# All chunks of U ahead of V, Wr in pieces ahead of its use, and more of the gather beside the routing

## The chip, the cores and the metric

The kernel runs on one core of a Trainium2 chip. A core has TensorE (PE) for matmuls, VectorE (DVE), ScalarE (ACT) and GpSimd (POOL) for the rest, and SyncE (SP), which here only issues DMAs; ACT and POOL issue some too. Each engine takes its instructions in order. The metric is the device time of one execution in microseconds (us).

## What is computed

The program is two transformer blocks over 512 tokens of width 1024. The change lies in the feed-forward of the first block, a mixture of 16384 experts with product keys:

```python
s = jnp.einsum('tpcd,pckd->tpck', q, sub_keys)      # 8 heads, 2 x 128 keys
...                                                   # top 16 of the sums: idx, top
g = jax.nn.softmax(top, axis=-1)
a = jax.nn.gelu(jnp.einsum('tpkd,td->tpk', u[idx], t))
return jnp.einsum('tpk,tpkd->td', g * a, v[idx])
```

Every token takes 8 x 16 of the 16384 rows of U and V (1024 wide, float32).

## The kernel before

The first 128 tokens (T0) are done by **gathering**: an indirect DMA on POOL (L1136) fetches one row of U or of V for each of the 128 tokens, 512 KB a load, 128 loads from each table. DVE multiplies a U row by the token's h (L1155, result `dots`) and adds a V row, weighted, to `accg` (L1160). Two loads and two such instructions are a pair of the generator `gathered`.

The other 384 tokens (TD) are done **densely**: all 16384 experts are worked through as 128 chunks of 128. For a chunk, `hidden` loads 512 KB of U (`w`, L1339), splits it into a high part on ACT (`wh`, L1342) and a low part on DVE (`wl`, L1343), runs 24 matmuls with 384 columns against the tokens (`hh`, `hl` of the pool h2, 32 KB a partition) and takes the gelu (`act`, L1351). `ahead` writes it to DRAM (`Ad`, L1357, 192 KB). Later `operands` reads it back (L1368), multiplies it by the routing weights `Wr` (L1372), splits it (`sh`, `sl`) and V's chunk (`vh`, `vl`, L132 and L134), and `products` adds 18 matmuls with 512 columns to six banks.

The weights come from the **routing**: for each of four blocks of 128 tokens `topk` finds the 16 best on DVE, and `spread` turns a block's choice (not the first's) into dense weights by one-hot products on PE (`go`, `oh`), which go to DRAM as `Wd`. `Wr` is the part of Wd for a group of 8 chunks (GROUP), 1.5 MB in 512-byte pieces, loaded when the first chunk of the group comes up (L1365).

So there are two stages. In the first, routing, 112 U chunks and the first gather pairs are woven together: each generator yields a number, and the one with the least sum goes next. A U chunk yields PACE, a gather pair GATHER; the routing's own numbers add up to 330. PE runs in this written order; the other engines' order is set by a scheduler. Four more U chunks (REST) follow. In the second stage the chunks 0 to 127 go through V; 116 (AHEAD) have their `act` in DRAM, the last 12 run `hidden` there. The remaining gather pairs are spread evenly over the first 120 chunks. Products trail the operands by OPS_LAG chunks.

SP's queue carries the loads of U, V, act and Wr in one order, and an entry that waits holds all behind it. The pool `st` has four buffers `w` (WBUFS) for U and V. `pm` holds Wr, act, sh, sl, vh, vl.

`rows_of` copies a vector that lies along partitions to all partitions as a row: it scales the identity by each of its 8 columns on DVE (`dg`, L372), multiplies by ones on PE and copies the bank (L374). It is used four times: gt1r, a2r, sh2r, and gt2r just ahead of the products with V. The vectors come from `late_mods`, which runs near the start beside the first projection and loads 32 pieces of `wmt` on SP.

Of the kernel before, what the change touches and what calls it, by code (L numbers as in the profile page):

```python
# [7 lines left out]
F32 = mybir.dt.float32  # L8
# [15 lines left out]
AHEAD = 116  # L24
REST = 4
PACE = 2.95
GROUP = 8
WBUFS = 4
# [4 lines left out]
GATHER = 11.0  # L33
OPS_LAG = 2
# [56 lines left out]
class Net:  # L91
# [271 lines left out]
    def rows_of(self, vec, name, pool):  # L363

        nc = self.nc
# [337 lines left out]
    def hg_chunks(self, hg, kv):  # L703
# [17 lines left out]
        for i in range(last + 2):  # L721
# [4 lines left out]
            else:  # L726
# [3 lines left out]
                self.gate = self.rows_of(self.gt1, "gt1r", ha)  # L730
# [290 lines left out]
    def peer(self):  # L1021
# [3 lines left out]
        a2 = self.gain_of(1, self.sc2, 0, "a2")  # L1025
        first = self.proj_first(self.ws, mv, lambda i: self.normed_half(i, [(hh, hl, a2)], 1e-6, self.sh2[:, :, 0]))
# [8 lines left out]
        self.Ad = self.tc.dram_tile([AHEAD, 128, TD], F32, name="Ad")  # L1035
        pg = self.pool("pg", "right")
        self.rows_natural(pg, a2)
        sc = self.queries(mv, first)
        pq = self.pool("pq", "right")
        ac = self.pool("ac")  # L1040
# [4 lines left out]
        gather = self.gathered(pg, ac)  # L1045
        with self.tc.manual_schedule(engines={mybir.EngineType.PE}):
            weave(self.route(pq, pg, sc), steps(ahead, AHEAD - REST), self.until_routed(gather))
# [12 lines left out]
        for e in range(128 + OPS_LAG):  # L1060
            if e < 128:
                ops[e] = self.operands(pm, e, dense)
# [13 lines left out]
        for name in ("pm", "pg", "h2"):  # L1076
            self.shut(name)
# [22 lines left out]
        self.shut("ac")  # L1100

    def rows_natural(self, pg, a2):
# [4 lines left out]
        gain, shift = self.rows_of(a2.unsqueeze(2), "a2r", tmp), self.rows_of(self.sh2, "sh2r", tmp)  # L1107
# [724 lines left out]
```

## Time and profile before

| | us |
|---|---|
| median of 3 runs | 3147.87 (3142.14 to 3153.35) |
| profiled execution, its own time | 3142.09 |
| its span | 3140.3 |
| routing beside U, from about 690 | to 1302 |
| products with V, to the last one | 1302 to 2007 |

The page gives busy time of each engine, a map of the span in 40 slices, the DMA queues, the chain that ended last, and the costliest groups of instructions by line. Busy shares over the whole span mix stages with different limits, so the rows further down are of stretches. A time in brackets is idle time of the engine, with what ended it. A wait for several things is put down to the one that came last; the profile names one DMA where an instruction waits for several.

### The profile page before, as it was taken

The numbers are of one execution on the slowest core, as the hardware profiler recorded it, in microseconds if no ns is written. First come the engines' busy times: TensorE is split into PE (matmuls) and PEld (weight loads), VectorE is DVE, ScalarE is ACT, GpSimd is POOL, SyncE is SP. The second block draws the span as 40 slices with busy tenths as digits, with TensorE's granted clock in tenths as the row PEclk, the third lists the DMA queues.
The fourth block names the chain that finished last, engine by engine and source line by source line (L and its number), as shares of the span: only waits on it lengthen the run. The fifth ranks groups of instructions, "written<-read, shape, count | busy, mean of one in ns | idle before, by whom it ended". The sixth has DMA issues, their size and how long they took to land.

```text
span 3140.3 us, 42392 instructions
## 1 busy us (share of the span) xinstructions
PE 2951.1 (94%) x16073; PEld 2529.5 (81%) x16073; DVE 1898.6 (60%) x3680; ACT 1268.6 (40%) x2275; POOL 401.1 (13%) x398
## 2 busy tenths in 40 slices
PE   7998999999999999898888888899999999999998
PEld 5887887799899999776676767778888887788887
DVE  5744497549999856678788875544433245543323
ACT  4233463343466778522232323432423234433222
POOL 2100000001111110133344431000000000000000
PEclk9999999999999999999999998999999999999999
DMA  6622202236676776899999995222333322123332
GB/s 250 228 64 72 62 1 81 98 126 202 204 239 218 255 248 225 286 353 358 355 363 360 361 353 201 64 72 94 100 95 94 99 86 65 54 88 94 99 103 81
DMA packets 257166, 537.79 MB, mean 171 GB/s; under 512 B 20161, under 2 KB 135105, under 8 KB 252609
## 3 DMA queue, kind: packets, MB, share of 16 engines
q1 hardware_dynamic: 196512, 345.82, 33.8%
q0 software_dynamic: 36864, 134.23, 12.0%
q10 hardware_dynamic: 23584, 55.03, 4.6%
q8 instruction: 126, 2.06, 0.3%
q14 instruction: 80, 0.65, 0.1%
HBM read 484.93 MB, written 50.08 MB: 170 GB/s over the span
## 4 chain that ended last, share of the span: by engine, by line
PE 56%; DVE 19%; DMA 9%; issue 4%; ACT 1%; POOL 1%; SPq 0%; DVEq 0%; ACTq 0%; POOLq 0%
PE bank L121 54%; DMA act<-Ad 7%; DVE wl L1343 2%; DVE gr L1155 2%; DVE accg L1160 2%; DVE vl L134 2%; DVE sl L134 1%; PE bank L608 1%; DVE act L1372 1%; PE bank L1471 1%; DVE idx L1275 1%; DVE tmp L1233 1%; DVE eq L1272 1%; DVE eq L1274 1%; DVE KX L802 1%
## 5 line engine op out<-in xcount | busy, mean ns | idle before, releaser
L121 PE MATMUL bank<-hh,wl 128*128 128x512 f32 (+2 forms) x2304 | 837.0, 364 | 41.8 <-DVE wl L1343 32.3
L121 PE MATMUL bank<-hh,wh 128*128 128x512 f32 (+2 forms) x2304 | 843.0, 367 | 16.2 <-ACT wh L1342 6.8
L121 PE MATMUL bank<-hl,wh 128*128 128x512 f32 (+2 forms) x2304 | 834.5, 362 | 1.5 <-DVE hl L271 0.8
L148 DVE TENSOR_TENSOR wl<-w,wh 128x1024 fp32r<-128x1024 f32 (+2 forms) x280 | 295.0, 1054 | 644.2 <-ACT wh L147 637.5
L147 ACT ACTIVATE wh<-w 128x1024 fp32r<-128x1024 f32 (+2 forms) x280 | 257.5, 920 | 746.1 <-PE bank L121 604.1
L121 PEld LDWEIGHTS bank<-hh,wl 128*128 128x128 f32 x2304 | 437.9, 190 | 101.0 <-DVE wl L1343 42.6
L121 PEld LDWEIGHTS bank<-hh,wh 128*128 128x128 f32 x2304 | 438.1, 190 | 69.9 <-ACT wh L1342 7.6
L121 PEld LDWEIGHTS bank<-hl,wh 128*128 128x128 f32 x2304 | 438.4, 190 | 48.9 <-DVE hl L532 1.6
L121 PE MATMUL bank<-vh,sh 128*128 128x512 f32 x768 | 248.7, 406 | 45.9 <-ACT sh L132 30.8
L121 PE MATMUL bank<-vl,sh 128*128 128x512 f32 x768 | 249.6, 407 | 19.4 <-DVE vl L134 19.2
L1136 POOL DMA_INDIRECT gr<-in_Un_dram,iu x128 | 170.6, 1333 | 735.7 <-DVE accg L1160 493.2
L121 PE MATMUL bank<-vh,sl 128*128 128x512 f32 x768 | 244.3, 400 | 0.0
L132 ACT ACTIVATE sh<-act 128x384 fp32r<-128x384 f32 x128 | 67.1, 525 | 383.4 <-DVE act L1372 347.3
L121 PEld LDWEIGHTS bank<-vh,sh 128*128 128x128 f32 x768 | 149.2, 196 | 80.6 <-ACT sh L132 33.8
L1343 DVE TENSOR_TENSOR wl<-w,wh 128x1024 fp32r<-128x1024 f32 x128 | 156.1, 1221 | 77.3 <-ACT wh L1342 77.3
L1342 ACT ACTIVATE wh<-w 128x1024 fp32r<-128x1024 f32 x128 | 135.1, 1056 | 163.8 <-PE bank L121 144.0
L121 PEld LDWEIGHTS bank<-vl,sh 128*128 128x128 f32 x768 | 149.1, 196 | 59.5 <-DVE vl L134 28.8
L121 PEld LDWEIGHTS bank<-vh,sl 128*128 128x128 f32 x768 | 150.4, 196 | 32.9 <-DVE sl L134 0.2
L1136 POOL DMA_INDIRECT gr<-in_V_dram,iv x128 | 151.4, 1183 | 172.4 <-DVE gr L1155 105.5
L134 DVE TENSOR_TENSOR vl<-w,vh 128x1024 fp32r<-128x1024 f32 x128 | 156.6, 1223 | 13.4 <-ACT vh L132 13.1
L1160 DVE SCALAR_TENSOR_TENSOR accg<-gr,wt,accg 128x1024 f32<-128x1024 f32 x127 | 162.8, 1282 | 0.2 <-DMA gr<-in_V_dram,iv 0.2
L1155 DVE SCALAR_TENSOR_TENSOR gr<-gr,h 128x1024 f32<-128x1024 f32 x128 | 156.0, 1221 | 2.8 <-DMA gr<-in_Un_dram,iu 2.8
(373 smaller groups left out, 4690.9 us busy)
## 6 DMA issues: line engine op xcount, KB each, us to landing
w<-in_U_dram SPq DMA_DIRECT2D x128, 512.0 KB, 4.6
w<-in_V_dram SPq DMA_DIRECT2D x128, 512.0 KB, 6.9
w<-in_wgu_dram SPq DMA_DIRECT2D x84, 512.0 KB, 3.5
Wd<-W ACTq DMA_DIRECT2D x24, 1024.0 KB, 6.8
Wr<-Wd SPq DMA_DIRECT2D x16, 1536.0 KB, 17.6
w<-in_wdown_dram SPq DMA_DIRECT2D x44, 512.0 KB, 3.6
Ad<-act ACTq DMA_DIRECT2D x116, 192.0 KB, 3.7
act<-Ad SPq DMA_DIRECT2D x116, 192.0 KB, 6.5
```

The costliest lines, as they stand in the source:

```text
L121: return self.nc.tensor.matmul(out, a, b, start=start, stop=stop)
L132: self.nc.scalar.activation(hi, src, AF.Copy)
L134: (low or self.nc.vector).tensor_tensor(out=lo, in0=src, in1=hi, op=OP.subtract)
L147: self.nc.scalar.activation(hi[:, :, :n], w[:, :, :n], AF.Copy)
L148: (self.low or self.nc.vector).tensor_tensor(out=lo[:, :, :n], in0=w[:, :, :n], in1=hi[:, :, :n], op=OP.subtract)
L608: nc.tensor.matmul(o, x[k], y[:, kk, :256], start=k == 0 and i == 0 and t % 2 == 0, stop=k == KC - 1 and i == 2, skip_group_check=True)
L802: nc.vector.tensor_tensor(out=half(KX[:, :, l], d), in0=half(e, d), in1=half(kt, d), op=OP.mult)
L1136: nc.gpsimd.indirect_dma_start(out=t, out_offset=None, in_=table, in_offset=bass.IndirectOffsetOnAxis(ap=idx, axis=0))
L1155: nc.vector.scalar_tensor_tensor(t, t, 1.0, self.h0, op0=OP.mult, op1=OP.mult, accum_out=dots[:, h, k:k + 1])
L1160: nc.vector.scalar_tensor_tensor(acc, t, wt[:, h, k:k + 1], acc, op0=OP.mult, op1=OP.add)
L1342: nc.scalar.activation(uh, w, AF.Copy)
L1343: nc.vector.tensor_tensor(out=ul, in0=w, in1=uh, op=OP.subtract)
```

## The change

The 12 U chunks that ran beside V move to the first stage: all 128 have their `act` in DRAM. PACE falls from 2.95 to 2.66, so that 124 of them fit into the same sum of the weave. GATHER becomes five numbers, one for each phase of the routing, which puts 40 of the 129 pairs beside the routing and leaves 89. The tokens' pool h2 is closed ahead of the products, and `pm` takes its room: act has 6 buffers instead of 3, the split pairs 6 instead of 4, OPS_LAG is 4. `Wr` is no longer loaded at its group's first chunk: `spread_rows` loads a sixth of the next group's Wr at each of the chunks 2 to 7 (WLATE) of a group. `rows_of` loses its matmuls: `late_mods` writes each vector to DRAM (`Rd`, 1024 numbers of 4 bytes) on SP, and `rows_of` reads it back to all partitions, on SP too. The gather pool `pg` changes its side and takes in `dots`, `wt` and `accg`.

```diff
-AHEAD = 116
 REST = 4
-PACE = 2.95
+PACE = 2.66
 GROUP = 8
+WLATE = 2
+ABUFS = 6
+VBUFS = 6
-GATHER = 11.0
-OPS_LAG = 2
+GATHER = (13.0, 13.0, 9.0, 6.0, 4.5)
+OPS_LAG = 4
...
-    def rows_of(self, vec, name, pool):
+    def keep_rows(self, n, vec):
+        self.nc.sync.dma_start(self.Rd[n].rearrange("(k p) -> p k", p=128), vec)
+
+    def rows_of(self, n, name, pool):
         o = pool.tile([128, D], F32, name=name)
-        for h in range(2):
-            b = self.bank()
-            for q in range(4):
-                k = h * 4 + q
-                dg = pool.tile([128, 128], F32, name="dg", bufs=2)
-                nc.vector.tensor_scalar(dg, self.ident, vec[:, k, 0:1], None, op0=OP.mult)
-                self.mm(b[:, q * 128:(q + 1) * 128], self.ones, dg, True, True)
-            nc.vector.tensor_copy(o[:, h * 512:(h + 1) * 512], b)
+        self.nc.sync.dma_start(o, self.Rd[n].partition_broadcast(128))
         return o
...
     def late_mods(self):
+        self.Rd = self.tc.dram_tile([4, D], F32, name="Rd")
...
+            if j in (2, 3, 5):
+                self.keep_rows((2, 3, 5).index(j) + (j > 2), t[:, :, 0])
+            if j == 4:
+                self.a2 = self.gain_of(1, t, 0, "a2")
+                self.keep_rows(1, self.a2)
...
-        self.Ad = self.tc.dram_tile([AHEAD, 128, TD], F32, name="Ad")
-        pg = self.pool("pg", "right")
+        self.Ad = self.tc.dram_tile([128, 128, TD], F32, name="Ad")
+        pg = self.pool("pg")
...
-            weave(self.route(pq, pg, sc), steps(ahead, AHEAD - REST), self.until_routed(gather))
+            weave(self.route(pq, pg, sc), steps(ahead, 128 - REST), self.until_routed(gather))
...
         self.shut("pa")
+        self.shut("h2")
         pm = self.pool("pm", "right")
         ar = self.pool("ar")
-        rows = self.rows_of(self.gt2, "gt2r", ar)
+        for i in range(GROUP - WLATE):
+            self.spread_rows(pm, 0, i)
+        rows = self.rows_of(3, "gt2r", ar)
...
             if n % 2:
-                yield GATHER
+                yield GATHER[self.phase]
...
         for t in range(5):
+            self.phase = t
...
-    def operands(self, pm, e, mv):
+    def operands(self, pm, e):
         nc, p = self.nc, self.p
-        if e % GROUP == 0:
-            self.Wr = pm.tile([128, TD // WT, GROUP, WT], F32, name="Wr", bufs=2)
-            nc.sync.dma_start(self.Wr, self.Wd[:, :, e:e + GROUP, :].rearrange("b p e t -> p b e t"))
-        if e < AHEAD:
-            a = pm.tile([128, TD], F32, name="act", bufs=3)
-            nc.sync.dma_start(a, self.Ad[e])
-        else:
-            a = self.hidden(pm, e, mv)
+        n, j = divmod(e, GROUP)
+        if j == 0:
+            self.Wr = self.Wn
+        a = pm.tile([128, TD], F32, name="act", bufs=ABUFS)
+        nc.sync.dma_start(a, self.Ad[e])
         a3 = a.rearrange("p (b t) -> p b t", t=WT)
         self.anchor = nc.vector.tensor_tensor(out=a3, in0=a3, in1=self.Wr[:, :, e % GROUP], op=OP.mult)
-        sh, sl = self.split(pm, a, [128, TD], "s", bufs=TAIL + OPS_LAG)
+        sh, sl = self.split(pm, a, [128, TD], "s", bufs=VBUFS)
         v = self.st.tile([128, 2, 512], F32, name="w", bufs=WBUFS)
         nc.sync.dma_start(v.rearrange("p a b -> p (a b)"), p['V'][e])
-        vh, vl = self.split(pm, v, [128, 2, 512], "v", bufs=TAIL + OPS_LAG)
+        if j >= WLATE and e < 128 - GROUP:
+            self.spread_rows(pm, n + 1, j - WLATE)
+        vh, vl = self.split(pm, v, [128, 2, 512], "v", bufs=VBUFS)
         return sh, sl, vh, vl
+
+    def spread_rows(self, pm, n, i):
+        if i == 0:
+            self.Wn = pm.tile([128, TD // WT, GROUP, WT], F32, name="Wr", bufs=2)
+        m = TD // WT // (GROUP - WLATE)
+        bs = slice(i * m, i * m + m)
+        self.nc.sync.dma_start(self.Wn[:, bs], self.Wd[bs, :, n * GROUP:(n + 1) * GROUP, :].rearrange("b p e t -> p b e t"))
```

Three places show what the scheduler makes of it. First the queue of SP at the start of the products with V (the number in a name tells buffers apart). Before:

```order
L1375 DMA w_13039<-in_V_dram 128x1024
L1365 DMA Wr_13017<-Wd_5521 128x24x128
L1368 DMA act_13019<-Ad_5522 128x384
L1368 DMA act_13032<-Ad_5522 128x384
L1368 DMA act_13051<-Ad_5522 128x384
L1375 DMA w_13058<-in_V_dram 128x1024
```

After:

```order
L1377 DMA w_13473<-in_V_dram 128x1024
L1389 DMA Wr_13396<-Wd_5499 128x4x128 x6
L372 DMA gt2r_13403<-Rd_646 128x1024
L1372 DMA act_13411<-Ad_5500 128x384
L1372 DMA act_13424<-Ad_5500 128x384
L1372 DMA act_13445<-Ad_5500 128x384
L1389 DMA Wr_13454<-Wd_5499 128x4x128
```

Four V chunks instead of two stand ahead of Wr, the row of gt2r stands ahead of the first act, and the second group's Wr begins at once.

Next the same queue in the middle of the stage, around the load of a group's Wr. Before:

```order
L1375 DMA w_13644<-in_V_dram 128x1024
L1368 DMA act_13598<-Ad_5522 128x384
L1365 DMA Wr_13853<-Wd_5521 128x24x128
L1368 DMA act_13637<-Ad_5522 128x384
L1375 DMA w_13681<-in_V_dram 128x1024
L1368 DMA act_13674<-Ad_5522 128x384
```

After:

```order
L1372 DMA act_14355<-Ad_5500 128x384
L1389 DMA Wr_14293<-Wd_5499 128x4x128 x2
L1377 DMA w_14330<-in_V_dram 128x1024
L1389 DMA Wr_14293<-Wd_5499 128x4x128
L1377 DMA w_14362<-in_V_dram 128x1024
L1372 DMA act_14393<-Ad_5500 128x384
L1389 DMA Wr_14293<-Wd_5499 128x4x128
L1372 DMA act_14431<-Ad_5500 128x384
L1389 DMA Wr_14293<-Wd_5499 128x4x128
L1377 DMA w_14400<-in_V_dram 128x1024
```

One entry of 1.5 MB has become six of 256 KB between the loads of V and act, and the last of the six stands ahead of the act of the group's first chunk (act_14501, some entries later).

Last DVE near the end of the stage. Before:

```order
L1343 TENSOR_TENSOR wl_17796<-w_17793,wh_17795 128x1024
L1372 TENSOR_TENSOR act_17700<-act_17700,Wr_17481 128x384
L134 TENSOR_TENSOR sl_17705<-act_17700,sh_17703 128x384
L134 TENSOR_TENSOR vl_17835<-w_17831,vh_17833 128x1024
L1343 TENSOR_TENSOR wl_17858<-w_17855,wh_17857 128x1024
```

After:

```order
L1374 TENSOR_TENSOR act_17799<-act_17799,Wr_17496 128x384
L136 TENSOR_TENSOR sl_17639<-act_17634,sh_17637 128x384
L136 TENSOR_TENSOR vl_17646<-w_17641,vh_17644 128x1024
L1374 TENSOR_TENSOR act_17830<-act_17830,Wr_17496 128x384
L136 TENSOR_TENSOR sl_17677<-act_17672,sh_17675 128x384
```

The low part of U (`wl`) is gone from here, and the multiply by Wr now stands several chunks ahead of the split of the same chunk. In DVE's order 73 gather instructions (43 on U rows, 30 on V rows) stand ahead of the first multiply by Wr where 45 (29 and 16) stood.

## Rows read from the trace of the kernel before

**Rows 1.** The page's first line.

```profile
span 3140.3 us, 42392 instructions
```

**Rows 2.** Stretches: length; busy (count) PE, PEld, DVE, ACT, POOL; PEclk, DMA share, GB/s.

```profile
690.00:843.00 153.00, 142.68 (x802) 137.55 (x801) 153.00 (x575) 54.71 (x73) 18.34 (x14) 1.00 0.60 193
...
843.00:1302.00 459.00, 443.27 (x2757) 434.99 (x2755) 360.41 (x808) 327.88 (x653) 56.09 (x41) 0.99 0.70 234
...
1350.00:1800.00 450.00, 397.80 (x1627) 318.91 (x1625) 363.98 (x498) 131.67 (x181) 183.33 (x152) 0.93 1.01 358
...
1890.00:2007.00 117.00, 109.54 (x539) 99.21 (x538) 67.39 (x80) 41.71 (x61) 14.12 (x10) 0.95 0.48 160
```

**Rows 3.** Timeline of DVE: start, length; two multiplies that waited (in brackets).

```profile
1396.96 0.56 DVE L1372 TENSOR_TENSOR act<-act,Wr 128x384 f32<-128x384 f32 x1 [8.13 <-DMA act<-Ad]
...
1438.01 0.56 DVE L1372 TENSOR_TENSOR act<-act,Wr 128x384 f32<-128x384 f32 x1 [7.68 <-DMA act<-Ad]
```

**Rows 4.** DVE by line, 1350-1800: count | busy, mean ns | idle.

```profile
L1160 DVE SCALAR_TENSOR_TENSOR accg<-gr,wt,accg 128x1024 f32<-128x1024 f32 x76 | 97.5, 1282 | 0.2 <-DMA gr<-in_V_dram,iv 0.2
L1155 DVE SCALAR_TENSOR_TENSOR gr<-gr,h 128x1024 f32<-128x1024 f32 x76 | 92.8, 1222 | 0.0
L1372 DVE TENSOR_TENSOR act<-act,Wr 128x384 f32<-128x384 f32 x89 | 49.3, 557 | 87.6 <-DMA act<-Ad 87.6
```

**Rows 5.** Waits of PE, 1317 to 1890: us in total, times, longest.

```profile
PE bank L121 <- ACT sh L132: 30.8, 7, 5.8
PE bank L121 <- DVE vl L134: 19.2, 11, 9.0
```

**Rows 6.** Short stretches: length, DVE busy on multiplies by Wr, PEclk, DMA share, GB/s.

```profile
1400.00:1420.00 20.00, 2.79 (x5) 0.89 0.96 340
1420.00:1440.00 20.00, 1.67 (x3) 0.96 1.06 377
1440.00:1456.00 16.00, 2.22 (x4) 0.83 0.92 319
1456.00:1480.00 24.00, 2.23 (x4) 0.99 1.06 381
```

**Rows 7.** DMA, 1350 to 1800: mean rate; Wr's issues, KB, us to landing.

```profile
DMA packets 81949, 161.25 MB, mean 358 GB/s; under 512 B 5462, under 2 KB 51239, under 8 KB 81923
...
Wr<-Wd SPq DMA_DIRECT2D x11, 1536.0 KB, 18.4
```

**Rows 8.** Waits of PE beside the routing, 690 to 1302.

```profile
PE bank L121 <- DVE wl L1343: 24.9, 27, 2.2
```

**Rows 9.** Timeline of PE: last products with U, products with V.

```profile
1289.86 0.34 PE L121 MATMUL bank<-hh,wh 128*128 128x384 f32 x1
...
1301.65 0.34 PE L121 MATMUL bank<-hh,wl 128*128 128x384 f32 x1
...
1313.39 1.20 PE L121 MATMUL bank<-dg,ones 128*128 128x128 f32 x4 [11.41 <-DVE dg L372]
...
1316.93 1.20 PE L121 MATMUL bank<-vh,sh 128*128 128x512 f32 x2
...
1325.53 0.62 PE L121 MATMUL bank<-vh,sh 128*128 128x512 f32 x2
...
1329.61 0.62 PE L121 MATMUL bank<-vh,sh 128*128 128x512 f32 x2
...
2006.71 0.61 PE L121 MATMUL bank<-vh,sl 128*128 128x512 f32 x2
```

**Rows 10.** Gather, 690-1302: length, DVE and POOL busy (count), PEclk, DMA share, GB/s.

```profile
690.00:1302.00 612.00, 58.85 (x82) 74.43 (x54) 0.99 0.67 224
```

**Rows 11.** The head: two DMA issues (100 to 150), one dg scaling on DVE.

```profile
w<-in_wmt_dram SPq DMA_DIRECT2D x18, 512.0 KB, 4.9
...
Ld<-lbm ACTq DMA_DIRECT2D x1, 8.0 KB, 3.2
...
L372 DVE TENSOR_SCALAR dg<-ident,a x8: 278/283/289, 555.0 to 566.2; 128x128 f32<-128x128 f32 x8
```

More of the change, by code (lines that the diff above doesn't have):

```diff
@@ L361, in gain_of @@
         return o
-    def rows_of(self, vec, name, pool):
-        nc = self.nc
+    def keep_rows(self, n, vec):
+        self.nc.sync.dma_start(self.Rd[n].rearrange("(k p) -> p k", p=128), vec)
+    def rows_of(self, n, name, pool):
         o = pool.tile([128, D], F32, name=name)
-        for h in range(2):
-            b = self.bank()
-            for q in range(4):
-                k = h * 4 + q
-                dg = pool.tile([128, 128], F32, name="dg", bufs=2)
-                nc.vector.tensor_scalar(dg, self.ident, vec[:, k, 0:1], None, op0=OP.mult)
-                self.mm(b[:, q * 128:(q + 1) * 128], self.ones, dg, True, True)
-            nc.vector.tensor_copy(o[:, h * 512:(h + 1) * 512], b)
+        self.nc.sync.dma_start(o, self.Rd[n].partition_broadcast(128))
         return o
@@ L729, in hg_chunks @@
                 wo = self.pool("wo")
-                self.gate = self.rows_of(self.gt1, "gt1r", ha)
+                self.gate = self.rows_of(0, "gt1r", ha)
                 self.mix_head(wo)
@@ L1024, in peer @@
         mv = ([hh[:, k] for k in range(KC)], [hl[:, k] for k in range(KC)])
-        a2 = self.gain_of(1, self.sc2, 0, "a2")
-        first = self.proj_first(self.ws, mv, lambda i: self.normed_half(i, [(hh, hl, a2)], 1e-6, self.sh2[:, :, 0]))
+        first = self.proj_first(self.ws, mv, lambda i: self.normed_half(i, [(hh, hl, self.a2)], 1e-6, self.sh2[:, :, 0]))
         self.finish = None
@@ L1034, in peer @@
         self.Wd = self.tc.dram_tile([TD // WT, 128, 128, WT], F32, name="Wd")
-        self.Ad = self.tc.dram_tile([AHEAD, 128, TD], F32, name="Ad")
-        pg = self.pool("pg", "right")
-        self.rows_natural(pg, a2)
+        self.Ad = self.tc.dram_tile([128, 128, TD], F32, name="Ad")
+        pg = self.pool("pg")
+        self.rows_natural(pg)
         sc = self.queries(mv, first)
         pq = self.pool("pq", "right")
-        ac = self.pool("ac")
         pa = self.pool("pa")
@@ L1044, in peer @@
         self.chosen = None
-        gather = self.gathered(pg, ac)
+        gather = self.gathered(pg)
         with self.tc.manual_schedule(engines={mybir.EngineType.PE}):
-            weave(self.route(pq, pg, sc), steps(ahead, AHEAD - REST), self.until_routed(gather))
+            weave(self.route(pq, pg, sc), steps(ahead, 128 - REST), self.until_routed(gather))
         self.shut("pq")
@@ L1061, in peer @@
             if e < 128:
-                ops[e] = self.operands(pm, e, dense)
+                ops[e] = self.operands(pm, e)
             want = left * min(e + 1, 120) // 120
@@ L1075, in peer @@
             self.products(banks, [t], held)
-        for name in ("pm", "pg", "h2"):
-            self.shut(name)
+        self.shut("pm")
         pt = self.xp = self.pool("pt", "right")
@@ L1099, in peer, with rows_natural @@
         self.shut("ar")
-        self.shut("ac")
-    def rows_natural(self, pg, a2):
+        self.shut("pg")
+    def rows_natural(self, pg):
         nc = self.nc
@@ L1106, in rows_natural @@
         tmp = self.pool("rn")
-        gain, shift = self.rows_of(a2.unsqueeze(2), "a2r", tmp), self.rows_of(self.sh2, "sh2r", tmp)
+        gain, shift = self.rows_of(1, "a2r", tmp), self.rows_of(2, "sh2r", tmp)
         r = self.rstd(self.ss[:, 0], 1e-6)
@@ L1122, in until_routed, with gathered @@
         self.gather_left = (256 + GAHEAD) // 2 - n
-    def gathered(self, pg, ac):
+    def gathered(self, pg):
         nc, p = self.nc, self.p
         iu, iv, g = self.chosen
-        dots = ac.tile([128, 8, 16], F32, name="dots")
-        wt = ac.tile([128, 8, 16], F32, name="wt")
-        self.accg = acc = ac.tile([128, D], F32, name="accg")
+        dots = pg.tile([128, 8, 16], F32, name="dots")
+        wt = pg.tile([128, 8, 16], F32, name="wt")
+        self.accg = acc = pg.tile([128, D], F32, name="accg")
         ring = {}
@@ L1354, in ahead @@
     def ahead(self, pool, mv):
-        for e in range(AHEAD):
+        for e in range(128):
             a = self.hidden(pool, e, mv)
```

## The prediction

> **What bounds the kernel now.** I read the map of the page first, then stretches around the change, then who waited for whom there. The span is 3140.3 us [rows 1]; the profiled execution's own time is 3142.09, and the median of the runs shown is 3147.87, 0.2% above it. The sum below is made against 3142.09 and then laid on the median. 0.3%, some 9 us, is about what a measurement of this kernel can tell from no change.
>
> Beside the routing (690 to 1302) PE is the bound: 142.7 + 443.3 of 612 us busy [rows 2], and what it waits for is nearly all `wl`, the low part of U on DVE, 24.9 us in 27 short waits [rows 8]. DVE is full up to 843 (153 of 153 us) and has 99 us free after that (360 of 459) [rows 2].
>
> The products with V run from 1302.0 to 2007.3 [rows 9], 705 us in three parts. First, 15 us in which PE has no product: the last U matmul starts at 1301.65, the `dg` of gt2r holds PE for 11.41 us, and the first product comes at 1316.93 [rows 9]. Then 573 us up to 1890, where no engine is full: PE 398 of 450 us, DVE 364, and DMA moves 358 GB/s at a share of 1.01 [rows 2, 7]. Last 117 us with the 12 late U chunks, where PE is nearly full (109.5) and DMA half idle (0.48, 160 GB/s) [rows 2].
>
> The middle part looks like a plain DMA bound, but the short stretches say otherwise. Two waits of DVE one group apart stand at 1396.96 and 1438.01, with 8.13 and 7.68 us ahead of them [rows 3]; waits on this multiply make 87.6 of DVE's 450 us [rows 4]. They are put down to act, but the act loads are small; every eighth multiply stalls, and that is the first of a group, which needs Wr. Wr takes 18.4 us to land [rows 7] and is asked for only a chunk or two ahead. So a group of eight takes 41.05 us: 33.4 us of unbroken work, 4.17 us a chunk, and 7.7 us of waiting. PE's waits for `sh` (30.8 us) and `vl` (19.2 us) [rows 5] follow from these. DMA has two levels in the same beat: 377 and 381 GB/s in the stretches that lead up to and hold the wait, 340 and 319 after it [rows 6], when buffers come free only as fast as DVE works.
>
> **The change part by part.** *U chunks.* Neighbouring U matmuls start 0.1734 us apart: 1289.86 to 1301.65 is 68 steps [rows 9]. 12 chunks of 24 are 49.9 us of PE. They leave the last 117 us and go to the routing, where PE is the bound. Of PE's 26 idle us there some should fill, since it now has more chunks between two spread steps; I take 5, so +45 us. The lower end is +38. The upper end is where the new DVE work is paid in series: 12 `wl` are within the U chunk's own time, but the order puts 28 more gather instructions ahead of the first multiply by Wr; at 1.25 us each [rows 4] that is 35 us, and the end is 50 + 35 = +85. I take a value near the lower end, because DVE has 99 us free after 843 and the new GATHER numbers put the added pairs late.
>
> *Products with V.* In the order Wr now comes in six entries of 256 KB ahead of the group that uses them, so the wait of 7.7 us a group goes. What is late next? Three prices for one chunk. DVE: 4.17 us of unbroken work now, less the gather that left. 54 loads stand before 1302 [rows 10], 40 pairs are 80 loads, so 26 loads and as many DVE instructions leave the stage; 0.83 pairs a chunk become 89/120 = 0.74, at 2.5 us a pair [rows 4], so 3.9 us. PE: one chunk of 18 matmuls takes 1329.61 - 1325.53 = 4.08 us [rows 9]. DMA: V 0.524 MB, act 0.197, an eighth of Wr 0.197, 0.74 pairs of 1.049 MB 0.778, together 1.696 MB; at the 379 GB/s of the stretches in which loads wait for nothing [rows 6] that is 4.47 us. So DMA becomes the bound, narrowly. I take 4.5 us. Ends: 4.74 us at the mean rate of 358 [rows 7], and 4.15 us, PE's 4.08 with small gaps, if DMA can give more. Six buffers for act and the pairs cost nothing in time; they let the loads run ahead, which the rate of 379 supposes.
>
> The trace shows no more than 381 GB/s over a beat [rows 6]. The Trainium skill (Perfetto Trace Analysis, Roofline) says that 358 GB/s is a core's share when both cores of a pair are at work, and that one alone may reach about 120% of it. By that rule, an estimate from its figures, a chunk's DMA takes 1.696 MB at 430 GB/s, 3.94 us, and PE is the bound; it is the second rival.
>
> *Start and end of the stage.* gt2r's matmuls go. In their place all of `pm` waits, because it lies in the room of h2, which the last U matmul reads; then Wr must land, and ACT and DVE must split. I take 11 us from the last U matmul to the first product in place of 15: one cold Wr with nothing queued ahead of it, less than its 18.4 us under load. The ends are 8 and 18. gt2r's load stands ahead of the first act on SP, and it waits for the last Ad write, 4 to 5 us; that lies beside Wr's landing. The last 8 chunks have no gather, so PE sets their pace: 8 x 4.08 = 33, and 3 us for the latency of the last splits. The stage: 11 + 120 x 4.5 + 33 + 3 = 587 us instead of 705, that is -118.
>
> *Rows by DRAM.* Three other uses of rows_of lose their `dg` work: 8 scalings of 0.283 us [rows 11] and two copies on DVE, and 8 short matmuls, at places where DVE or PE is nearly full; 2 us each, -6. Against that, late_mods' four writes stand in SP's queue behind a load of `wmt` that has to land (4.9 us) [rows 11] and be used; each holds the loads behind it, but four buffers `w` lie ahead of PE. I take +3, between 0 and 16 (all four seen by PE in full, 4 us each). A write of small pieces stands in the trace, Ld, 8 KB, 3.2 us to landing [rows 11]; nobody waits for Rd until hundreds of us later. Sum -3, from -6 to +10.
>
> On such writes the Trainium skill speaks against the change: DMA: Bandwidth & Descriptors, Specifications, says that below 512 bytes a transfer is done as read-modify-write. An estimate from that page, 1024 pieces counted as 512 bytes each, makes a write as dear as a load of `wmt`, and the sum would be up to 20 us worse; the landing of Ld shows no sign of that, and no row has pieces of 4 bytes.
>
> Sum: +45 - 118 - 3 = -76 us, 3142.09 - 76 = 3066; on the median 3147.87 - 76 = **3072 us**.
>
> **The rivals.** (a) *DMA stays at 358 GB/s.* For it: a share of 1.01 over 450 us. Against it: the two levels within a beat. 120 x 0.24 = 29 us less gain: 3101. (b) *PE becomes the bound.* DMA gives what is asked once loads run ahead; 120 x 0.35 = 42 us more gain: 3030. For it: DVE and PE both have a lower price than DMA at 379, and PEclk, 0.93 now [rows 2], would rise with fewer gaps. Against: no stretch of 20 us shows such a rate. (c) *The routing pays DVE's work too.* PE waits for `wl` behind gather instructions in DVE's order: +85 instead of +45, so 40 less gain: 3112. For it: DVE is full until 843 and PE's waits there are all for `wl` [rows 8]. Against: the free 99 us. (d) *Slower: Wr's pieces come late.* Each group waits for its last piece. The gain is gone when the stage takes 705 - 42 = 663 us, a chunk 5.13, that is a wait of (5.13 - 3.9) x 8 = 10 us a group, against 7.7 now. At 13 us, between that and a full landing of 18.4 [rows 7], a chunk takes 5.5 us: 120 x 1.0 = 122 us lost, 3194. For it: six more entries in a queue in which one holds all. Against: in the order the last piece stands some chunks of V ahead of its use. That the change doesn't do what it says is ruled out by the order for the gather (73 instead of 45) and the U chunks.
>
> **How the numbers follow.** The forecast 0.42, (a) 0.20, (b) 0.13, (c) 0.18, (d) 0.07. The predicted time is the forecast's, 3072. Around it the open costs (38 to 50 in the routing, 8 to 18 at the start, -6 to +10 for the rows) give some +-20. With (a) and (c) and part of them together the upper end is 3122, and (b) with a few us spare gives 3035 as the lower; (d), the rest of (b) and (a) with (c) in full stay outside. Faster by over 0.3%: all but (d) and the worst mixtures of (a) and (c), 0.89; within 0.3% 0.05; slower 0.06.
>
> **What would show it.** Right: in the products with V no wait of 7 us on every eighth multiply; multiplies by Wr 4.5 us apart; DMA at 370 to 385 GB/s over the whole stretch; the last U matmul at about 1344 and the last product at about 1930, 587 us later; beside the routing 80 gather loads and PE still over 94% busy. DMA at 358 with PE waiting shows (a), PE full at 4.1 us a chunk (b), longer waits for `wl` beside the routing (c), waits on the first multiply of a group of over 10 us (d). I am wrong altogether if some new wait, at the room of h2 or on the writes of Rd, costs tens of us.

## The result and the profile after

The changed kernel takes 3178.59 us (median of 4 runs, 3176.20 to 3179.77), the kernel before 3148.79 us beside it: a ratio of 1.0095, interval 1.0076 to 1.0115. It is slower by 0.95%, some 30 us, where 76 us less were forecast. The profiled execution has a span of 3174.4 us, 34.1 more than [rows 1].

Four markers cut the span into parts: the first gelu of a U chunk, the last U matmul, the last product with V, and the end. The groups below are the ACT line that makes act, its first and last start, of before and of after; then the last U matmul, the first product and the last one of after (columns: start, duration, engine, line, operation, out and in, count, idle time ahead of it and who ended it).

```profile
L1351 ACT ACTIVATE act<-bank x128: 463/473/502, 695.6 to 1995.9; 128x384 f32<-128x384 f32 x128
```

```profile
L1356 ACT ACTIVATE act<-bank x128: 458/473/496, 736.4 to 1403.7; 128x384 f32<-128x384 f32 x128
```

```profile
1403.35 0.34 PE L123 MATMUL bank<-hh,wl 128*128 128x384 f32 x1
1413.97 1.22 PE L123 MATMUL bank<-vh,sh 128*128 128x512 f32 x2 [10.28 <-ACT sh L134]
...
2033.95 0.61 PE L123 MATMUL bank<-vh,sl 128*128 128x512 f32 x2
```

The markers of before are 695.6, 1301.65 and 2006.71 [rows 9]. So:

| part, us | before | after | difference | forecast |
|---|---|---|---|---|
| to the first gelu of U (the head) | 695.6 | 736.4 | +40.8 | -3, with the other places of rows_of |
| from there to the last U matmul (routing) | 606.1 | 667.0 | +60.9 | +45 |
| from there to the last product (stage of V) | 705.1 | 630.6 | -74.5 | -118 |
| the rest | 1133.6 | 1140.4 | +6.9 | 0 |
| span | 3140.3 | 3174.4 | +34.1 | -76 |

All three forecast parts missed in the same direction. The stage of V falls in two. These are the busy times of after by stretch, first beside the routing and then in the stage (columns: stretch, length, busy time of PE, weight loads, DVE, ACT and POOL with counts, granted clock of PE, DMA share, GB/s); they answer to [rows 2].

```profile
736.00:843.00 107.00, 99.34 (x549) 94.70 (x548) 107.00 (x463) 39.68 (x54) 8.37 (x6) 0.99 0.56 184
843.00:1403.00 560.00, 534.84 (x3264) 525.57 (x3264) 446.16 (x935) 357.04 (x693) 108.72 (x76) 0.99 0.73 251
1420.00:1750.00 330.00, 304.42 (x1291) 243.65 (x1290) 279.59 (x386) 109.42 (x148) 150.62 (x112) 0.97 1.04 380
1750.00:1950.00 200.00, 161.45 (x651) 128.05 (x650) 140.17 (x190) 52.58 (x74) 71.90 (x55) 0.92 0.90 310
```

Up to 1750 DMA moves 380 GB/s at a share of 1.04, as forecast. From 1750 it moves 310 at 0.90, PE is idle a fifth of the time and DVE three tenths. Something new sets the pace there. The head has a sign of its own: the four writes of Rd, 4 KB each, take 11 to 14 us to land, and while they are under way stretches of 5 us move as little as 26 to 55 GB/s. First the DMA issues of after between 85 and 200 (KB each, median us to landing), then four such stretches, the columns as above.

```profile
Rd<-gt SPq DMA_DIRECT2D x2, 4.0 KB, 12.7
Rd<-sh SPq DMA_DIRECT2D x1, 4.0 KB, 11.1
...
Rd<-a SPq DMA_DIRECT2D x1, 4.0 KB, 12.0
```

```profile
90.00:95.00 5.00, 5.00 (x31) 4.40 (x30) 1.91 (x4) 0.63 (x1) 0.00 (x0) 1.00 1.25 143
95.00:100.00 5.00, 5.00 (x30) 4.35 (x29) 0.00 (x0) 0.00 (x0) 0.00 (x0) 1.00 1.06 52
125.00:130.00 5.00, 5.00 (x24) 4.14 (x23) 0.42 (x3) 0.00 (x0) 0.00 (x0) 1.00 0.77 55
150.00:155.00 5.00, 0.89 (x18) 0.65 (x12) 0.46 (x3) 0.00 (x0) 0.00 (x0) 1.00 0.44 26
```

In the stretch at 95 DMA's share is 1.06 while 52 GB/s flow. The share counts the time of the packets that start in a stretch, and the pieces of 4 bytes start in the stretch before it. These are the packets of the two stretches, 90 to 95 and 95 to 100:

```profile
DMA packets 1229, 0.71 MB, mean 143 GB/s; under 512 B 1056, under 2 KB 1056, under 8 KB 1229
DMA packets 109, 0.26 MB, mean 52 GB/s; under 512 B 9, under 2 KB 9, under 8 KB 109
```

So what takes long just after the pieces are the packets of the loads: 0.78 us each in the mean from 95 to 100 (a share of 1.06 of 16 engines over 5 us, 109 packets), against 0.16 us from 140 to 145 (464 packets, a share of 0.93). By what the pieces hold them is not shown. The loads come late. These are the longest waits of after between 85 and 200 (engine, line, waited for: us in total, times, longest), and under them the rows of before that name the same loads:

```profile
ACT wh L149 <- DMA w<-in_win_dram: 53.6, 5, 21.0
DVE mscr L333 <- DMA w<-in_wmt_dram: 36.1, 8, 10.4
```

```profile
ACT wh L147 <- DMA w<-in_win_dram: 9.8, 2, 5.8
DVE mscr L331 <- DMA w<-in_wmt_dram: 8.0, 8, 2.0
```

### The profile page after: what moved, and what is told of

Same layout as the page of the kernel before. It is cut to its first block, busy times and chain, and to the rows that moved or that the text cites. A ratio compares the mean times of both kernels' runs of the same rounds, so it can differ in the third digit from the quotient of the medians.

```text
span 3174.4 us, 42523 instructions
## 1 busy us (share of the span) xinstructions
PE 2956.9 (93%) x16009; PEld 2530.6 (80%) x16009; DVE 1888.4 (59%) x3640; ACT 1267.7 (40%) x2275; POOL 427.4 (13%) x398
## 5 line engine op out<-in xcount | busy, mean ns | idle before, releaser
L123 PE MATMUL bank<-hh,wl 128*128 128x512 f32 (+2 forms) x2304 | 841.2, 366 | 43.2 <-DVE wl L1348 26.6
L123 PE MATMUL bank<-hh,wh 128*128 128x512 f32 (+2 forms) x2304 | 846.9, 368 | 21.0 <-ACT wh L149 10.4
L1140 POOL DMA_INDIRECT gr<-in_Un_dram,iu x128 | 195.6, 1528 | 669.1 <-DVE accg L1164 462.2
L134 ACT ACTIVATE vh<-w 128x1024 fp32r<-128x1024 f32 x128 | 135.2, 1059 | 311.8 <-DMA w<-in_V_dram 311.8
```

What stands on the lines that cost most here:

```text
L123: return self.nc.tensor.matmul(out, a, b, start=start, stop=stop)
L134: self.nc.scalar.activation(hi, src, AF.Copy)
L1140: nc.gpsimd.indirect_dma_start(out=t, out_offset=None, in_=table, in_offset=bass.IndirectOffsetOnAxis(ap=idx, axis=0))
```

## The experiments

The first theory was two separate costs: the writes of Rd in the head, and in the stage of V something that throttles the loads from 1750 on. Each is taken away by itself, and the first is also added by itself to the kernel before. Ratios are to the kernel before, run beside each.

### The writes of Rd

**no_rd**: the old way to spread the four vectors, all else as changed.

```
-        self.nc.sync.dma_start(o, self.Rd[n].partition_broadcast(128))
...
+                dg = pool.tile([128, 128], F32, name="dg", bufs=2)
+                nc.vector.tensor_scalar(dg, self.ident, vec[:, k, 0:1], None, op0=OP.mult)
+                self.mm(b[:, q * 128:(q + 1) * 128], self.ones, dg, True, True)
...
-                self.keep_rows((2, 3, 5).index(j) + (j > 2), t[:, :, 0])
...
-                self.keep_rows(1, self.a2)
```

> The changed kernel with the old way to spread gt1, a2, sh2 and gt2 over the partitions (scalings on VectorE, matmuls with ones), so nothing is written to Rd; all else as in the changed kernel. Theory (the four writes of Rd in 4-byte pieces stop the loads of the head): the first gelu of U comes at 695 to 700 us instead of 736, the whole 35 to 42 us shorter than the changed kernel, near 3138. Rival (the head is late for another reason in the new order, for instance because a2 is made early): the first gelu stays near 736 and the time near 3175.

Measured: 3139.48 us, ratio 0.9985 (0.9971 to 1.0), against 1.0095 with the writes: 1.1% or 35 us. The first gelu of U starts at 701.5. The theory holds; the rival's 736 does not appear.

**before_rd**: the kernel before with the writes and broadcast loads alone.

```
+            if j in (2, 3, 5):
+                self.keep_rows((2, 3, 5).index(j) + (j > 2), t[:, :, 0])
+            if j == 4:
+                self.a2 = self.gain_of(1, t, 0, "a2")
+                self.keep_rows(1, self.a2)
```

> The kernel before with one part of the change alone: the four vectors go to Rd in 4-byte pieces and come back by broadcast loads. Theory: about 41 us slower than the kernel before in the head, some 5 us won back where the dg matmuls and scalings fall away, so 3180 to 3190. Rival (the writes only hurt together with the rest of the change): 3140 to 3150.

Measured: 3181.27 us, ratio 1.0119 (1.0092 to 1.0146), and a first gelu at 728.0, 32 us later. This part alone costs the kernel before as much as the whole change does, 37 us. The time lies in the range written, but not by its reasons alone. The fallen dg work does come back where gt2r's matmuls held PE: from the last U matmul (1332.85) to the first product (1335.84) it takes 3.0 us instead of 15.3. The products then take 20 us longer than before (1335.84 to 2045.80, against 689.8 us [rows 9]); why is open.

**rd_turned**: the same writes at the same place of the same queue, in pieces of 512 bytes.

```
-        self.nc.sync.dma_start(self.Rd[n].rearrange("(k p) -> p k", p=128), vec)
+        b = self.bank()
+        self.nc.tensor.transpose(b[:KC, :128], vec, self.ident)
+        o = self.rt
+        self.nc.vector.tensor_copy(o, b[:KC, :128])
+        self.nc.sync.dma_start(self.Rd[n].rearrange("(k p) -> k p", p=128), o)
```

> The changed kernel with each vector turned on TensorE to 8 rows of 128 before the write, so that a write of Rd is 8 pieces of 512 bytes instead of 1024 of 4 bytes; same queue, same place in the order. Theory (the size of the pieces is the cost): first gelu of U at 697 to 702, time near 3140, as without the writes or a little better. Rival (the cost is the place of the write in SP's queue, which waits there for VectorE while loads stand behind it): the first gelu stays at 725 to 740 and the time within 10 us of the changed kernel.

Measured: 3145.61 us, ratio 1.0005 (0.9992 to 1.0017), first gelu at 701.7, as without the writes. The place in SP's queue is not what costs; the size of the pieces is. The busy times between 85 and 175 us say the same, first of after, then of rd_turned, the columns as above: PE is busy 63 of 90 us against 80, at a granted clock of 0.83 against 0.94.

```profile
85.00:175.00 90.00, 63.27 (x311) 51.10 (x310) 51.54 (x111) 14.98 (x25) 2.16 (x3) 0.83 0.73 170
```

```profile
85.00:175.00 90.00, 79.82 (x492) 67.01 (x492) 63.45 (x131) 23.12 (x44) 6.77 (x6) 0.94 0.60 197
```

The time of rd_turned is 28 us below the changed kernel's by the ratios and 6 above no_rd's; the profiled executions of rd_turned and no_rd part in the stage of V (638 against 631 us), not in the head.

### The order of the multiply

In VectorE's order of the changed kernel I counted, ahead of the multiply of act by Wr of chunk e, how many chunks' low parts (sl) had not been made yet, that is, by how many chunks the multiply runs ahead of the split of the same act:

```
chunk           0   25   50   55   70   80   90  100  110  120
before          0    0    0    0    0    0    0    0    0    0
after           0    0    0    1    3    4    5    4    5    4
near1           0    0    0    0    0    0    0    0    0    0
act9            0    0    0    1    3    4    5    6    7    7
```

With 6 buffers and a lead of 5 every buffer of act is taken when a multiply is done; the room for the next act comes free only with the sl that stands between the two multiplies, and its load leaves SP behind that sl. The trace shows the loop. Below, DVE in after, where a multiply at 1818.31 has waited 6.42 us for its act and the sl that frees a room follows it; then what DVE and SP waited for between 1750 and 1950; then the act loads of that stretch and those of 1420 to 1750 (KB each, median us to landing).

```profile
1818.31 0.56 DVE L1374 TENSOR_TENSOR act<-act,Wr 128x384 f32<-128x384 f32 x1 [6.42 <-DMA act<-Ad]
1818.79 0.55 DVE L136 TENSOR_TENSOR sl<-act,sh 128x384 fp32r<-128x384 f32 x1
1819.26 1.28 DVE L1164 SCALAR_TENSOR_TENSOR accg<-gr,wt,accg 128x1024 f32<-128x1024 f32 x1
1820.45 1.22 DVE L136 TENSOR_TENSOR vl<-w,vh 128x1024 fp32r<-128x1024 f32 x1
```

```profile
DVE act L1374 <- DMA act<-Ad: 55.4, 21, 7.3
...
SPq L1372 <- DVE sl L136: 93.0, 32, 8.6
```

```profile
act<-Ad SPq DMA_DIRECT2D x36, 192.0 KB, 5.5
```

```profile
act<-Ad SPq DMA_DIRECT2D x72, 192.0 KB, 10.4
```

After 1750, 36 acts in 200 us are 5.6 us each, about the 5.5 us that one takes to land: close to one landing after the other. Before 1750, 72 in 330 us are 4.6 us each though one takes 10.4 us to land, because several are under way.

**near1**: Rd as changed, the multiply of chunk e held behind sl of chunk e-1.

```
-        self.anchor = nc.vector.tensor_tensor(out=a3, in0=a3, in1=self.Wr[:, :, e % GROUP], op=OP.mult)
+        if e >= 1:
+            with self.after(self.lows[e - 1]):
+                self.anchor = nc.vector.tensor_tensor(out=a3, in0=a3, in1=self.Wr[:, :, e % GROUP], op=OP.mult)
...
+        self.lows.append(self.low_ins)
```

> The changed kernel, Rd as it is, with the multiply of act by Wr of chunk e held behind the low part (sl) of chunk e-1 in VectorE's order. In the changed kernel it stands up to 5 chunks ahead from the middle of the products on, with 6 buffers of act. Theory (an act load can then be asked for only one chunk ahead, so VectorE waits for it and DMA falls from 380 to 310 GB/s after 1750): DMA stays at 375 to 385 GB/s to the end of the gather, the stage falls from 638 to some 595 to 605 us, the time to 3135 to 3145. Rival (DMA falls for another reason, such as ScalarE's order of V and sh): rate and time stay as in the changed kernel, 3170 to 3180.

Measured: 3126.28 us, ratio 0.9944 (0.9926 to 0.9962); against the changed kernel's 1.0095 that is 1.5%, 47 us. The last U matmul starts at 1401.88 and the last product at 1985.63: a stage of 584 us instead of 630.6, also 47 us less. The time is lower than I had written by 9 us and the stage by 11; the place is right. The same two stretches of the stage, of near1:

```profile
1420.00:1750.00 330.00, 308.85 (x1319) 249.94 (x1318) 278.16 (x382) 107.86 (x146) 144.08 (x108) 0.97 1.03 371
1750.00:1950.00 200.00, 189.78 (x807) 150.70 (x806) 173.38 (x228) 67.92 (x91) 89.36 (x64) 0.99 1.04 382
```

From 1750 DMA gives 382 GB/s instead of 310, and PE's busy time goes from 161 to 190 of 200 us. The multiply's wait for act, 55.4 us above, is gone: this is near1's group of its line from 1403 on (busy us, mean ns, idle before).

```profile
L1377 DVE TENSOR_TENSOR act<-act,Wr 128x384 f32<-128x384 f32 x127 | 70.1, 552 | 0.0
```

**act9**: the changed kernel with 9 buffers of act and the order left to itself.

```
-ABUFS = 6
+ABUFS = 9
```

> The changed kernel with 9 instead of 6 buffers of act and nothing else; in VectorE's order the multiplies then stand up to 8 chunks ahead. Theory (it is the order that eats the room, whatever its size): an act load is still asked for one chunk ahead of its multiply late in the stage; DMA falls as before after about 1800, and at most 15 us are gained: 3162 to 3180. Rival (6 buffers are too few): as with the multiply held back, 3120 to 3135.

Measured: 3160.35 us, ratio 1.0057 (1.004 to 1.0074), 12 us less than the changed kernel by the ratios and 2 us below the range written. The lead goes on to 8 and the rate falls later, after 1850. More room without an order is used up by the order:

```profile
1750.00:1850.00 100.00, 87.41 (x360) 69.18 (x360) 79.39 (x110) 29.63 (x42) 42.86 (x32) 0.94 1.03 372
1850.00:1950.00 100.00, 80.49 (x313) 63.29 (x314) 75.05 (x95) 29.22 (x41) 35.50 (x26) 0.89 0.86 296
```

### Both at once

**nord_near1**: no writes of Rd, and the multiply held back.

```
-            if j in (2, 3, 5):
-                self.keep_rows((2, 3, 5).index(j) + (j > 2), t[:, :, 0])
...
+            with self.after(self.lows[e - 1]):
```

> The changed kernel with both causes taken away: no writes of Rd (the old way to spread the four vectors) and the multiply of chunk e held behind the low part of chunk e-1. Theory (two separate costs, some 39 us in the head and some 52 us in the products with V): they add, 3085 to 3095, faster than the kernel before by 1.6 to 2%. Rival (they overlap, since a shorter head moves the same wait elsewhere): 3105 to 3125.

Measured: 3093.5 us, ratio 0.9839 (0.9822 to 0.9855). The two costs add within the spread. The span is 3095.4, 44.9 less than [rows 1], and its parts are: first gelu at 699.5 (+3.9), last U matmul at 1368.74 (routing 669.2, +63.2), last product at 1955.35 (stage 586.6, -118.5), the rest 1140.0 (+6.5).

The next two ask what in the products with V brought this gain.

**nord_near1_wlate**: Wr in one load at the start of its group.

```
         if j == 0:
-            self.Wr = self.Wn
+            self.Wr = pm.tile([128, TD // WT, GROUP, WT], F32, name="Wr", bufs=2)
+            nc.sync.dma_start(self.Wr, self.Wd[:, :, e:e + GROUP, :].rearrange("b p e t -> p b e t"))
...
-        if j >= WLATE and e < 128 - GROUP:
-            self.spread_rows(pm, n + 1, j - WLATE)
```

> As nord_near1, but Wr in one load, asked for with the first act of its group as in the kernel before; with 6 buffers of act that is now about 5 chunks (some 22 us) ahead of its use. Theory (the pieces ahead of the group remove the wait of 7.7 us a group): the wait comes back in part, 3120 to 3190. Rival (the depth of the act buffers alone puts Wr early enough, the pieces add nothing): within 8 us of nord_near1, and no wait on every eighth multiply.

Measured: 3104.69 us, ratio 0.9872 (0.9856 to 0.9889), 11 us more than nord_near1: between the two expectations and near the rival. No multiply waits any more, without the pieces.

The run also shows what the wait of the kernel before was, and it is not what the prediction and this expectation say. First the multiplies of before that start ahead of the one that waits at 1396.96 [rows 3], then SP of before at the load of Wr ahead of that wait (start and duration of the issue), then SP, ACT and DVE of nord_near1_wlate around such a load.

```profile
L1372 DVE TENSOR_TENSOR act<-act,Wr x18: 551/556/562, 1302.9 to 1384.3; 128x384 f32<-128x384 f32 x18
```

```profile
1376.33 0.46 SPq L1365 DMA_DIRECT2D Wr<-Wd  x1
1377.65 10.65 SPq L1368 DMA_DIRECT2D act<-Ad  x1
```

```profile
1450.36 0.37 SPq L1370 DMA_DIRECT2D Wr<-Wd  x1
1451.50 8.38 SPq L1382 DMA_DIRECT2D w<-in_V_dram  x2
...
1468.21 1.06 ACT L134 ACTIVATE vh<-w 128x1024 fp32r<-128x1024 f32 x1 [10.69 <-DMA w<-in_V_dram]
...
1472.29 0.56 DVE L136 TENSOR_TENSOR sl<-act,sh 128x384 fp32r<-128x384 f32 x1 [9.83 <-ACT sh L134]
```

18 multiplies stand ahead of the one that waits, so it is that of chunk 18, the third of its group; of the 113.8 us that the multiplies of before wait in the stage, 96.9 stand at the third of a group. The Wr issued at 1376.33 is first used at 1421.41, 45 us later, though the program asks for it at its group's first chunk; so Wr is not late. The act behind it on SP is: its issue takes 10.65 us, and behind the 14 loads of Wr from 1337 on it takes 8.9 us in the mean, where the median issue of an act takes 0.34. So the wait is put down rightly to act, which stands behind the 1.5 MB of Wr. In nord_near1_wlate Wr is asked for as early (issued 1450.36, first used 1494.86) and holds the entry behind it as long, 8.5 us in the mean. With 6 buffers of act that entry is now a load of V, and the wait comes at vh and after it at sl. DVE's waits of over 3 us between 1380 and 1900 add up to 98 us in before, 67 here and 34 in nord_near1: the depth of act has shortened and moved the wait, and the pieces take half of what is left.

**nord_near1_act3**: Wr in pieces, 3 buffers of act.

```
-ABUFS = 6
+ABUFS = 3
```

> As nord_near1, Wr in six pieces ahead of its group, but 3 buffers of act as in the kernel before. Theory (Wr's lateness was what stalled the kernel before, so with Wr early the depth of act hardly matters): within 10 us of nord_near1, 3090 to 3103. Rival (the depth of act was what counted, the act load asked for two chunks ahead comes late by itself): 3125 to 3170, with waits for act or sh on most chunks.

Measured: 3119.08 us, ratio 0.9915 (0.9894 to 0.9935), 24 us more than nord_near1 by the ratios, between the two expectations as well. The multiplies wait for act again, 45.8 us between 1420 and 1880, about half of the 87.6 in 450 us of before [rows 4]:

```profile
DVE act L1377 <- DMA act<-Ad: 45.8, 17, 6.0
```

So what stalled the kernel before was the one large entry of Wr ahead of an act with three buffers, and not a late Wr. With the other cure in place the depth of act is worth more (24 us) than the pieces (11 us). No run has the rest of the change with neither, so what the two bring together is not shown.

### Where the gather lies

**nord_near1_g11**: one pair every 11 units beside the routing, as before, so 14 more pairs in the stage of V.

```
-GATHER = (13.0, 13.0, 9.0, 6.0, 4.5)
+GATHER = (11.0,) * 5
```

> As nord_near1, with one gather pair for every 11 units beside the routing as in the kernel before, so that some 14 pairs more lie beside the products with V. Theory (the products are bound by DMA at about 380 GB/s): 14 pairs of 1.05 MB are 39 us more there, and the routing gets only 5 to 12 us shorter: 3112 to 3125. Rival (a pair costs as much beside the routing, where it takes VectorE from the low parts of U): within 8 us of nord_near1.

Measured: 3152.22 us, ratio 1.0029 (1.0018 to 1.004): 59 us more than nord_near1, outside both expectations. The routing is 20 us shorter (first to last gelu 696.9 to 1346.5, 649.6 us, against 699.5 to 1369.1, 669.6), and the stage of V 76 us longer (663 against 587). So it pays twice the 39 us of its bytes. DMA is slower as well: 343 GB/s at a share of 0.97 between 1420 and 1880, first row, against 372 at 1.02 in nord_near1, second row. ACT waits 259 us for V there, against 135; why V comes later with the same buffers is open.

```profile
1420.00:1880.00 460.00, 386.77 (x1568) 304.43 (x1567) 357.61 (x488) 131.86 (x179) 219.09 (x148) 0.93 0.97 343
```

```profile
1420.00:1880.00 460.00, 427.01 (x1807) 341.17 (x1806) 390.21 (x535) 150.72 (x204) 214.53 (x152) 0.98 1.02 372
```

**nord_near1_gmore**: the other way, some 11 more pairs beside the routing.

```
-GATHER = (13.0, 13.0, 9.0, 6.0, 4.5)
+GATHER = (13.0, 13.0, 8.0, 4.5, 3.0)
```

> As nord_near1, with the steps of the gather beside the routing shorter late in it (8.0, 4.5, 3.0 for 9.0, 6.0, 4.5), so that some 11 more pairs lie beside the routing. From nord_near1_g11 against nord_near1, 14 pairs cost the routing 20 us and took 73 us off the products. Theory (the products are still bound by DMA at 380 GB/s): 11 pairs take 11 x 1.05 MB at 380 GB/s = 30 us off the products and cost 16 us, 3075 to 3085. Rival (the products are by now bound by TensorE, 4.08 us a chunk against 4.5): they take 20 us off at most and the routing pays as much or more, 3090 to 3105.

Measured: 3076.26 us, ratio 0.9769 (0.9752 to 0.9787), the fastest here, 2.3% below the kernel before. The routing takes 688.7 us (gelu 700.4 to 1389.1), 19 more, and the stage some 38 less. The time is the theory's, but its reason is no longer the whole one: PE is busy 451 of 460 us, so it is PE that bounds the stage now. That further pairs would bring little follows from this row, but no run tries it:

```profile
1420.00:1880.00 460.00, 450.69 (x1967) 367.37 (x1966) 394.05 (x537) 162.04 (x220) 203.78 (x141) 1.00 1.04 376
```

### One queue or all

**near1_rd_act**: near1 with the 4-byte writes issued by ScalarE.

```
-        self.nc.sync.dma_start(self.Rd[n].rearrange("(k p) -> p k", p=128), vec)
+        self.nc.scalar.dma_start(self.Rd[n].rearrange("(k p) -> p k", p=128), vec)
```

> As near1, with the four writes of Rd, in 4-byte pieces as in the change, issued by ScalarE instead of SP. Theory (the pieces keep the 16 DMA engines busy, so loads from any queue crawl while they last): the head stays late, first gelu of U at 720 to 740, time 3115 to 3130. Rival (only what stands behind them in SP's own queue is held): the first gelu comes at 700 or so, time 3088 to 3098 as without the writes.

Measured: 3119.86 us, ratio 0.9908 (0.9891 to 0.9926), first gelu at 732.4. Some 11 us of the cost go away by the ratios, 3 by the first gelu (735.2 in near1). That time alone would not tell theory and rival apart, since ScalarE now also waits for a vector that it has to write, third row below. The waits for the loads on SP do tell them apart. First near1, then near1_rd_act, 85 to 200:

```profile
DVE mscr L333 <- DMA w<-in_wmt_dram: 31.1, 8, 10.1
```

```profile
DVE mscr L333 <- DMA w<-in_wmt_dram: 34.7, 8, 9.9
ACT F L580 <- DVE gt L334: 18.0, 1, 18.0
```

The loads on SP are as late as in near1 though the writes stand in another queue.

## Why the prediction was wrong

**Rows by DRAM: the writes were priced at +3 us and cost 35.** The sum had -3 for the whole part, with +10 as the worst end. The step that failed is "I take +3, between 0 and 16", from the landing of Ld [rows 11]. Ld's 8 KB go in longer pieces, two of 32 bytes to a partition; Rd's 4 KB go in 1024 pieces of 4. The row was the nearest by bytes, and bytes were not what is paid for: the four writes put 35 us on the path (no_rd against after, in the time and at the first gelu), about 9 us a write, and the same bytes in pieces of 512 have their first gelu 35 us earlier. The 41 us of the head of after against before hold some 6 more that no_rd has too. The cover that I named, four buffers w ahead of PE, was not enough, as the waits for win and wmt show. The Trainium skill (DMA: Bandwidth & Descriptors, Specifications) spoke of read-modify-write below 512 bytes; the estimate from it, up to 20 us worse, had the right sign and was too low here. I set it aside for a row that had no pieces of that size, and should at least have let it into the range.

**Products with V: the price was right, two steps under it were not.** The stage gave -74.5 instead of -118. The step that failed and cost the time is "Six buffers for act and the pairs cost nothing in time; they let the loads run ahead". They let them run ahead only while the multiply stays close to its split. From chunk 55 on it doesn't, which the order of the changed kernel shows and I hadn't counted: the multiplies wait 55.4 us for act from 1750 to 1950, and DMA gives 310 GB/s instead of 379. With that one thing set right the stage measures 584 (near1) and 586.6 us (nord_near1) against the forecast of 587, and DMA gives 380 GB/s in after's first part against 379. These terms carry the price of 4.5 us a chunk: 72 acts in 330 us of after are 4.6. From the last U matmul to the first product it is 10.6 us in after against 11, and 11.3 in nord_near1, where the dg work stands there again.

The second step is the reading of the wait: "every eighth multiply stalls, and that is the first of a group, which needs Wr", and Wr "is asked for only a chunk or two ahead". It is the third of a group, Wr is asked for 45 us ahead, and the act behind it is late (nord_near1_wlate). That the cure fitted this other cause as well, since the pieces and the depth both bring that act sooner, is luck.

The agreement to a microsecond is luck too, and the price does not hold for any number of pairs. By the same sum, with 103 pairs or 78 in the stage instead of 89, an estimate from 1.049 MB a pair at 379 GB/s, the stage would be 623 us in nord_near1_g11 and 554 in nord_near1_gmore; 663 and 549 were measured. What adds 40 us in the first is open.

**Rivals.** (a) and (b) were about the rate of DMA. Over 100 us no run here moved more than 388 GB/s, and with the order mended DMA gives 382 GB/s from 1750 to 1950 (near1), so (a)'s 358 is not its level. (b)'s full PE appears only in nord_near1_gmore, by taking load away from DMA, not by more from it. By the rule of the Trainium skill (Perfetto Trace Analysis, Roofline), some 430 GB/s for a core alone, more would have been left; here 424 flow over 11 us at the start of the kernel (nord_near1, 10.5 to 21.5), but over 100 us no run shows more than those 388. (d) asked for a wait on the first multiply of a group; the wait that came was on more than half of the late ones (21 of the 37 between 1750 and 1950), for act, and with another cause.

**Routing: mis-sized by 16 us.** +45 became +60.9, inside its ends of 38 and 85. The term is the gather beside the routing, put into DVE's free time at nothing. nord_near1_g11 parts it: with the pairs at the old pace the 12 U chunks cost 649.2 - 606.1 = 43 us (last U matmul at 1346.14), near the forecast's 45, and the 14 pairs 20 us more. PE is the bound there: its waits for `wl` are 16.6 us in nord_near1_g11 and 26.6 in nord_near1, and its busy time goes from 629 to 637 us for as many matmuls, at a granted clock of 0.98 instead of 0.99. So rival (c) is in part right, 16 of its 40 us; that the gather instructions ahead of a `wl` make these waits, as it says, is argued and not shown.

**The rest: +6.9 us**, for which the sum had no term. It is 1139 to 1140 us in every kernel with the changed stage and 1133 in before_rd as in before, so it comes neither from the writes nor from the order of the multiply. It lies right behind the last product: DVE's first step there, which needs no product, starts 7.4 us ahead of the last product in before and 1.2 us ahead of it in after, where it has waited for PE. Before, then after:

```profile
1999.27 1.29 DVE L1090 TENSOR_TENSOR y<-accg,gt2r 128x512 f32<-128x512 f32 x2
```

```profile
2032.79 1.29 DVE L1094 TENSOR_TENSOR y<-accg,gt2r 128x512 f32<-128x512 f32 x2 [9.86 <-PE bank L123]
```

By the program `y` now lies in the room of `pm`, which the last products read; that this is the reason is argued, no run moves it. Without the writes the head is also 1 to 6 us later than before (696.9 to 701.8 in the six kernels without them, against 695.6, one profiled execution each); that is open.

The closing words named "some new wait, at the room of h2 or on the writes of Rd" as what would make it wrong altogether. The second came, at 9 us a write, and the stage's own new wait on top.

## What to carry to other kernels

Price a DMA by its pieces, not by its bytes: a small write in 4-byte pieces holds up large loads, of its own queue and of another, and one transpose on TensorE that makes its pieces 512 bytes long takes the cost away. More buffers let loads run ahead only if the order of the engine that uses them stays near the instruction that frees them; count in the order how far the user runs ahead of the releaser, and hold it back if that comes near the number of buffers. Before naming what a wait is for, count which chunk waits and look what stands ahead of its load in the queue. Where a stage is bound by DMA and another by TensorE with VectorE partly free, moving loads from the one to the other paid here until TensorE bounded both.

## What the hardware showed that I had not expected

- A write of 4 KB in 1024 pieces of 4 bytes takes 11 to 14 us to land in the middle of the loads, and DMA's share stands at 0.8 to 1.25 while 52 to 143 GB/s flow; the packets of loads that start just behind the pieces take 0.78 us instead of 0.16. The loads of 512 KB back from Rd to all partitions, by broadcast, land in 3.7 to 5.2 us.
- The writes hold up loads of another queue as much as those of their own: DVE waits 34.7 us for wmt with the writes in ScalarE's queue and 31.1 with them in SP's (8.0 without them, in before).
- Behind a load of 1.5 MB in 512-byte pieces the next issue on SP takes 8.9 us in the mean (before) where 0.34 us is the median.
- Loads of act land in 10.4 us (median) when many are under way and in 5.5 us when each waits for the one before; the second is the slower way to work, 5.6 us a chunk against 4.6.
- In the head PE's granted clock is 0.83 in the mean between 85 and 175 us in after, where its weights come late, and 0.94 in rd_turned. In after it is at 0.50 to 0.54, the lower of its two levels, from 155 to 175 us; PE is busy 0.9 of 5 us from 150 to 155 and not at all in the next 5.
